# Sample attention in blocks of 16 rows by 8 columns, with queries and keys made four token tiles at a time

## The chip, the cores and the metric

The kernel runs on one core of one Trainium2 chip. The metric is device time in microseconds (us). A core has five engines that run in parallel, each with its own instruction stream in a fixed order: TensorE (PE in the profile; PEld is its weight load), VectorE (DVE), ScalarE (ACT), GpSimd (POOL) and SyncE (SP), which here only issues DMA transfers. They wait for one another through semaphores. An instruction that waits holds up everything behind it in its own stream.

## The reference

One layer of a hybrid encoder, with the same weights for a prompt of 512 tokens and a sample of 1024 tokens, model width 1024, in float32:

```python
h = rms_norm(x, norm_g)
u_pool, g_pool, q, k, v, g_attn = split(h @ w_in)          # 6 x 512 columns
pool_out = pool_mixer(u_pool, w_pool, pool_scale) * silu(g_pool)
q = rms_norm(q per head, q_norm_g) * HEAD_DIM ** -0.5       # 8 heads of 64
k = rms_norm(k per head, k_norm_g)
attn = neighbourhood_attention(q, k, v, rpb) * silu(g_attn)
y = x + concat(pool_out, attn) @ w_out
```

The neighbourhood attention sees the tokens as a grid 64 columns wide: 8 rows in the prompt, 16 in the sample. A query at row r and column c attends to 8 rows (r - 4 to r + 3, clamped at the borders) by 16 columns (c - 8 to c + 7, clamped), with a learned bias for each head, row offset (15) and column offset (31). For the prompt the 8 rows are all the rows there are.

## The kernel before

Nothing is put to an engine directly. Each operation is recorded with a priority and a modelled duration, and a planner (`Plan.order`) then lays out the fixed order of every engine: attention and evictions have priority over the long products, which run in the order of the code and fill what is left of TensorE. The planner adds a margin (`TO_PE`, 800 ns) before it counts on a result of another engine on TensorE. All instructions are issued in one place, so nearly all bear one line number; groups are told apart by the names of their tiles.

float32 values are carried as pairs of a high and a low float32r part. A product of two such pairs takes three matmuls (high by high, high by low, low by high), which is `mm3`. For the scores, queries hold the high part of a head in 64 partitions and the low part in the other 64, so two matmuls are enough: one against the high part of the keys (`k[hd]`, in both halves), one against their low part (`k[2 + hd]`).

The heads are taken in four pairs, first all of the sample, then all of the prompt. For a pair, `project_qkv` computes q, k and v token tile by token tile (128 tokens; tiles `acc`, 24 matmuls of 384 columns each). Two token tiles make a group: ScalarE brings each out of PSUM (`qkv`), the squares are summed per head, a chain of 12 small VectorE operations on `st4` (128x8) makes the reciprocal roots, q and k are scaled, TensorE transposes them into one PSUM bank (`ptq`: q in the first half, k in the second), and four evictions per head write the bank to `q` and `k`: ScalarE writes the high parts, VectorE the low parts (`low`). The sample has four such groups per pair, the prompt two. The v parts go through DRAM (`vd`) and come back as tiles of 128 keys (`vs`): for each group of 4 rows, four tiles of 4 rows by 32 columns that overlap in columns.

`attention` then runs, per head, over two query row tiles (`rt`, 8 rows each) and four column blocks (`cb`, 16 columns each): a block is 128 queries. In the sample its keys are 12 rows by 32 columns (24 at the borders, so 288 columns of scores and not 384). For each block `head_rows` does: two score matmuls (`s`); a VectorE pass that adds the bias and takes the row minimum of the negative (`ns`); ScalarE's exp with its sum; reciprocal; a scaling; three transposes (`pt`); the eviction into high and low (`pp`, two operations of 384 columns); three matmuls with v (`po`). Every two blocks the result is added up (`pv`) and multiplied into the gate (`sg`).

The bias tables are built once on GpSimd from `rpb` and stored in DRAM (`tab`). Per head and row tile they are read back with 6 or 7 DMAs, since the rows a query may see differ; the parts of the tile that no DMA writes hold -1e30 from the start. Two bias tiles are used, one for each row tile.

After the attention of a pair the rest of the pair's products follows (`accu`, `accg`: 24 matmuls of 512 columns each) and the pooling (`accm`). At the end come the output products (`acco`).

Of the kernel before, what the change touches and what calls it, by code (L numbers as in the profile page):

```python
# [24 lines left out]
P = 128  # L25
# [4 lines left out]
HD = 64  # L30
# [5 lines left out]
CT = (2, 1, 1, 0)  # L36
BANKS = dict(acc=3, s=2, pt=2, po=1)
# [301 lines left out]
def encoder(ctx, tc, xn_p, xt_p, xn_s, xt_s, w_in, w_out, w_pool, pscale, ng, qg, kg,  # L339
# [26 lines left out]
    qk_t = sb.tile([P, 2], F32, name="qk_t")  # L366
    gqk = sb.tile([P, 1], F32, name="gqk")
# [12 lines left out]

    HR = 8 * 15
    tab = dram.tile([32, HR, 32], F32, name="tab")

    def build_table():
        rel = ring("pv", 1, [P, 80], "rel")
        sp.dma_start(out=rel[0:HR, 0:48], in_=rpbm.rearrange("h r c -> (h r) c"))
        sp.dma_start(out=rel[0:HR, 48:79], in_=rpb.rearrange("h r c -> (h r) c"))

# [14 lines left out]
    def bias_rows(out, h, ro, q0, nq, a):  # L403

        o = tab.offset + (h * 15 + ro) * 32
        if nq == 1:
            sp.dma_start(out=out[16 * q0:16 * q0 + 16, :, a:a + 256],
                         in_=bass.AP(tab.tensor, o, [[HR * 32, 16], [8 * HR * 32, 3], [1, 256]]))
            return
        for ct in range(3):  # L410
            sp.dma_start(out=out[16 * q0:16 * (q0 + nq), ct, a:a + 256],
                         in_=bass.AP(tab.tensor, o + ct * 8 * HR * 32, [[32, nq], [HR * 32, 16], [1, 256]]))

    def load_bias(bt, kind, h):
        if kind == "all":
            bias_rows(bt, h, 0, 0, 8, 0)
        elif kind == "top":
            bias_rows(bt, h, 3, 3, 5, 0)
            for q in range(3):
                bias_rows(bt, h, 3, q, 1, (3 - q) * 32)  # L420
        else:
            bias_rows(bt, h, 0, 0, 4, 128)
            for q in range(4, 8):
                bias_rows(bt, h, 3, q, 1, (7 - q) * 32)
# [63 lines left out]
    ns_edge = {cb: sb.tile([P, 384], F32, name=f"ns_edge_{cb}") for cb in (0, 3)}  # L488
# [4 lines left out]
    class Sequence:  # L493


        def __init__(self, sq, S, kt_rows, hts, Rb):
            self.sq, self.S, self.kt_rows, self.hts, self.Rb = sq, S, kt_rows, hts, Rb
            self.NT, self.NB, self.CH, self.KEYS = S // P, S // 512, kt_rows // 4, kt_rows * 32
# [58 lines left out]
        def project_qkv(self, p, w, group=1):  # L557
# [3 lines left out]
            for t0 in range(0, self.NT, 2):  # L561
                st4 = ring("st4", 2, [P, 4, 8], f"st4_{sq}_{p}_{t0}")
                qkvs = []
                for t in (t0, t0 + 1):
# [28 lines left out]
                rsqrt(st4[:, 2], st4[:, 3], st4[:, 1])  # L593
                pt = bank("pt", f"ptq_{sq}_{p}_{t0}")
                for i, t in enumerate((t0, t0 + 1)):
# [7 lines left out]
                    pe.transpose(pt[:, i * P:(i + 1) * P], in_=qkv[:, 0:P], identity=ident)  # L603
                    pe.transpose(pt[:, 256 + i * P:256 + (i + 1) * P], in_=qkv[:, P:256], identity=ident)
# [4 lines left out]
                rt, r0 = (2 * t0) // 8, (2 * t0) % 8  # L609
                lo, hi = 7 - r0, 3 - r0  # L610
                qa = slice(base + rt * 512, base + (rt + 1) * 512)
                ka = slice(base + t0 * P, base + t0 * P + 256)
                own = [slice(hd * HD, hd * HD + HD) for hd in range(2)]
                k_src = [pt[own[hd], 256:512] for hd in range(2)]
                q_src = [pt[own[hd], 0:256].rearrange("p (r cb c) -> p r cb c", r=4, cb=4) for hd in range(2)]
                q_dst = []
                for hd in range(2):
                    for rows in (own[hd], own[1 - hd]):
                        v = q[hd][rows, qa].rearrange("p (cb r c) -> p r cb c", cb=4, r=8)
                        q_dst.append(v[:, lo::-1, :, ::-1] if hi < 0 else v[:, lo:hi:-1, :, ::-1])  # L620
                for hd in range(2):
                    for rows in (own[hd], own[1 - hd]):
                        act.activation(out=k[hd][rows, ka], in_=k_src[hd], func=AF.Copy, scale=gqk[own[hd]])
                    act.activation(out=q_dst[2 * hd], in_=q_src[hd], func=AF.Copy)
                for hd in range(2):
                    low(k[2 + hd][own[hd], ka], k_src[hd], k[hd][own[hd], ka], gqk[own[hd]])
                    low(q_dst[2 * hd + 1], q_src[hd], q_dst[2 * hd])
                rg = t0 // 2
                for cb in range(4):
                    sa = bass.AP(vd.tensor, vd.offset + (rg * 4 * GW + C0[cb]) * 256,  # L630
                                 [[GW * 256, 4], [256, 32], [1, 256]])
                    sp.dma_start(out=vs[base // 256 + rg][:, cb].bitcast(F32), in_=sa)
# [11 lines left out]

        def attention(self, p):
            for hd in range(2):
                for rt in range(self.NB):
                    h = 2 * p + hd
                    kind, i = (("top", 0), ("bot", 1))[rt] if self.S == 1024 else ("all", h % 2)
                    bt = bias[i][:, 0:3 * self.KEYS].rearrange("p (t c) -> p t c", t=3)  # L650
                    load_bias(bt, kind, h)
                    self.head_rows(p, hd, rt, bt)

        def head_rows(self, p, hd, rt, bt):
            sq, KEYS, base = self.sq, self.KEYS, self.base(p)
# [418 lines left out]
```

## Time and profile before

| | |
|---|---|
| Time, median of 3 runs (lowest to highest) | 648.9 us (647.37 to 649.58) |
| The profiled execution: its own time | 648.4 us |
| The profiled execution: its span | 646.6 us |
| Instructions in the span | 11390 |
| DMA, mean over the span | 157 GB/s |

The span runs from the first to the last instruction of the profile, and 1.8 us of the profiled execution's own time lie around it. Durations in the next parts are from this one execution. In a row that groups instructions, "busy" is the union of their intervals and "mean" the mean length of one. Matmuls overlap (a mean of 399 ns can go with one start every 230 ns), so what a matmul costs TensorE is read from the distance between starts. A figure after "idle" is the time for which the engine had nothing to do just before these instructions, with what ended it.

### The profile page before, as it was taken

How to read it: one execution, taken by the hardware profiler on the slowest of the kernel's cores; microseconds unless marked ns; L12 is line 12 of the kernel's file. 1: busy time of each engine (PE TensorE's matmuls, PEld its weight loads, DVE VectorE, ACT ScalarE, POOL GpSimd, SP SyncE). 2: the span in 40 equal slices, each digit the busy share in tenths (PEclk: the TensorE clock that was granted, in tenths of full speed). 3: DMA queues.
4: the chain of work that ended last, by engine and by line, in shares of the span. 5: the costliest groups of instructions: out<-in, count | busy, mean ns of one | idle time of the engine just before them, and what ended most of it. 6: DMA issues, size and time to landing. Idle time of an engine off the chain costs nothing.

```text
span 646.6 us, 11390 instructions
## 1 busy us (share of the span) xinstructions
PE 635.0 (98%) x3404; PEld 567.0 (88%) x3404; DVE 557.1 (86%) x1647; ACT 372.8 (58%) x910; POOL 100.6 (16%) x142
## 2 busy tenths in 40 slices
PE   6999999999999999999999999999999999999997
PEld 5998899988899888999889989899899878887886
DVE  6688999899987999967999989989999989879742
ACT  5766786568656476544777556477566457323210
POOL 1130100000000000101001110021212423405412
PEclk9999999999999999999999999999999999999999
DMA  8974354442274522425344355545556687843631
GB/s 304 348 205 143 104 169 124 123 121 79 59 246 137 182 62 69 134 95 152 127 112 143 109 168 162 174 139 144 169 174 195 189 261 231 269 152 118 191 131 65
DMA packets 92961, 101.53 MB, mean 157 GB/s; under 512 B 12900, under 2 KB 78564, under 8 KB 92900
## 3 DMA queue, kind: packets, MB, share of 16 engines
q1 hardware_dynamic: 92900, 100.81, 50.7%
q8 instruction: 27, 0.44, 0.3%
q14 instruction: 34, 0.28, 0.1%
HBM read 81.41 MB, written 19.37 MB: 156 GB/s over the span
## 4 chain that ended last, share of the span: by engine, by line
PE 91%; DVE 4%; DMA 3%; issue 1%; ACT 0%; SPq 0%; DVEq 0%; ACTq 0%
PE acc_s L330 21%; PE acco L330 15%; PE accg_s L330 14%; PE acc_p L330 10%; PE accu_s L330 7%; PE accg_p L330 6%; PE po_s L330 4%; PE accu_p L330 3%; PE pt_s L330 3%; PE s_s L330 3%; DMA xr<-in_xn_s 1%; PE po_p L330 1%; PE ptq_s L330 1%; DVE B L330 1%; PE pt_p L330 1%
## 5 line engine op out<-in xcount | busy, mean ns | idle before, releaser
L330 PE MATMUL acc_s<-w_sA,ht_s 128*128 128x384 f32 x768 | 145.9, 342 | 6.3 <-DVE w_sA L330 6.3
L330 PEld LDWEIGHTS acc_s<-w_sA,ht_s 128*128 128x128 f32 x768 | 136.0, 190 | 7.6 <-ACT ht_s L330 5.9
L330 PE MATMUL accg_s<-ht_s,w_sT 128*128 128x512 f32 x384 | 100.4, 399 | 0.0
L330 PEld LDWEIGHTS accg_s<-ht_s,w_sT 128*128 128x128 f32 x384 | 70.0, 188 | 12.0
L330 PE MATMUL acc_p<-w_pA,ht_p 128*128 128x384 f32 x384 | 75.4, 339 | 0.7 <-DVE w_pA L330 0.5
L330 PEld LDWEIGHTS acc_p<-w_pA,ht_p 128*128 128x128 f32 x384 | 66.1, 188 | 1.8 <-DVE w_pA L330 0.8
L330 PE MATMUL acco<-B,left 128*128 128x512 f32 x228 | 56.2, 395 | 0.6 <-DVE left L330 0.6
L330 PE MATMUL accu_s<-ht_s,w_sT 128*128 128x512 f32 x192 | 53.0, 400 | 0.0
L330 PEld LDWEIGHTS acco<-B,left 128*128 128x128 f32 x228 | 41.9, 188 | 9.5 <-DVE left L330 1.0
L330 PE MATMUL accg_p<-ht_p,w_pT 128*128 128x512 f32 x192 | 47.6, 395 | 0.0
L330 PEld LDWEIGHTS accg_p<-ht_p,w_pT 128*128 128x128 f32 x192 | 35.3, 188 | 6.9
L330 ACT ACTIVATE k<-ptq_s,gqk 64x256 fp32r<-64x256 f32 x64 | 30.1, 470 | 18.8 <-PE ptq_s L330 18.1
L330 PEld LDWEIGHTS accu_s<-ht_s,w_sT 128*128 128x128 f32 x192 | 34.6, 188 | 5.1
L330 DVE TENSOR_TENSOR xr<-acco,xr 128x512 f32<-128x512 f32 x30 | 20.5, 686 | 20.4 <-PE acco L330 18.2
L330 ACT ACTIVATE ns_edge<-ns_edge,sm_s 128x288 f32<-128x288 f32 x54 | 28.4, 529 | 16.5 <-DVE sm_s L330 16.3
L330 ACT ACTIVATE ns_s<-ns_s,sm_s 128x384 f32<-128x384 f32 x53 | 31.7, 610 | 10.1 <-DVE sm_s L330 9.9
L330 DVE TENSOR_TENSOR pp_s<-pt_s,pp_s 128x384 fp32r<-128x384 f32 x64 | 34.5, 544 | 0.3
L330 PE MATMUL po_s<-pp_s,v 128*128 128x256 f32 x192 | 32.0, 287 | 0.0
L330 PE MATMUL s_s<-k,q 128*128 128x288 f32 (+1 forms) x128 | 31.4, 330 | 0.0
L330 PEld LDWEIGHTS po_s<-pp_s,v 128*128 128x128 f32 x192 | 28.9, 188 | 1.5
L330 POOL TENSOR_TENSOR vt_s<-qkv_s,vt_s 128x128 fp32r<-128x128 f32 x17 | 9.1, 540 | 122.0 <-ACT vt_s L330 97.3
L330 ACT ACTIVATE qkv_s<-acc_s,rr_s 128x384 f32<-128x384 f32 x24 | 13.7, 578 | 23.6 <-PE acc_s L330 20.9
(221 smaller groups left out, 1350.4 us busy)
## 6 DMA issues: line engine op xcount, KB each, us to landing
v<-vd_s SPq DMA_DIRECT2D x64, 128.0 KB
wr_sA<-in_w_in SPq DMA_DIRECT2D x32, 192.0 KB
wr_sT<-in_w_in SPq DMA_DIRECT2D x32, 192.0 KB
wr_pA<-in_w_in SPq DMA_DIRECT2D x32, 192.0 KB
wr_pT<-in_w_in SPq DMA_DIRECT2D x32, 192.0 KB
out<-xr SPq DMA_DIRECT2D x24, 256.0 KB
x<-in_xt_s SPq DMA_DIRECT2D x16, 256.0 KB
vd_s<-vt_s SPq DMA_DIRECT2D x32, 128.0 KB
```

What stands on the lines that cost most here:

```text
L330: op.fn()
```

## The change

- **Blocks.** A sample block is now 16 rows (all of them) by 8 columns. Its keys are all 16 rows of the columns that its queries can see: 23 columns (368 scores) in the middle, 16 columns (256 scores) in the first and the last block. That is three chunks of 128 keys for six of the eight blocks of a head and two for the other two. Queries and keys of the sample are stored column by column, with the 16 rows innermost, so the evictions write with a step of 16 elements (64 bytes), and the keys of a block are one contiguous strip. The gate's product `sg` now runs down columns, with a step of 64 elements.
- **v.** The sample's v comes back as eight tiles of 8 columns by 16 rows that don't overlap: 8 DMAs for a pair and not 16, all of them after the last token tile. Two of the four `vs` buffers serve one pair, the other two the next.
- **Bias.** The sample has tables of its own in DRAM (`tab_s`, two of them), with a row for each query row and all masked places written out. They are built with one TensorE transpose, copies on GpSimd and 10 DMAs, 64 bytes in a run for eight of these. A head reads its bias with 3 DMAs and not 13. The tile per head alternates.
- **Groups.** q and k are made in groups of four token tiles: two PSUM banks (`qt`, `kt`), one `st4` chain of 128x16 per group, evictions of 512 elements. The sample has two groups per pair, the prompt one.
- **The rest.** `ns` tiles are four fixed ones, cleared at the start and, for two of them, again before the prompt; the bias tiles are no longer filled with -1e30 at the start; the mixed result of a head is stored with one DMA and not two. The prompt's blocks are computed as before.

```diff
+KS = 16 * 23
+EDGE = 256
...
+        rt_ps, rt = bank("pt", "rel_t"), ring("tree", 2, [P, 528], "rel_ts")
+        pe.transpose(rt_ps[0:32, 0:HR], in_=rel[0:HR, 48:80], identity=ident[0:HR, 0:HR])
+        act.activation(out=rt[0:32, 0:HR], in_=rt_ps[0:32, 0:HR], func=AF.Copy)
...
+            for dst, step, src, move, n in ((56, 15, 3, 0, 9), (192, 16, 4, 1, 4), (8, 16, 0, 1, 3)):
+                pool.tensor_copy(out=at(t, dst, [256, 2], [step, n]), in_=at(rt, 15 * h + src, [15, 2], [move, n]))
...
-            for t0 in range(0, self.NT, 2):
-                st4 = ring("st4", 2, [P, 4, 8], f"st4_{sq}_{p}_{t0}")
+            for t0 in range(0, self.NT, 4):
+                st4 = ring("st4", 2, [P, 3, 16], f"st4_{sq}_{p}_{t0}")
...
-                    pe.transpose(pt[:, i * P:(i + 1) * P], in_=qkv[:, 0:P], identity=ident)
-                    pe.transpose(pt[:, 256 + i * P:256 + (i + 1) * P], in_=qkv[:, P:256], identity=ident)
+                    pe.transpose(qt[:, i * P:(i + 1) * P], in_=qkv[:, 0:P], identity=ident)
+                    pe.transpose(kt[:, i * P:(i + 1) * P], in_=qkv[:, P:256], identity=ident)
...
+                def k_block(x):
+                    return x[:, qa] if self.S == 512 else x.rearrange("p (c r) -> p r c", r=16)[:, r0:r0 + 8]
...
+                for hd in range(2):
+                    act.activation(out=q_dst[2 * hd], in_=q_src[hd], func=AF.Copy)
+                    low(q_dst[2 * hd + 1], q_src[hd], q_dst[2 * hd])
                 for hd in range(2):
                     for rows in (own[hd], own[1 - hd]):
+                        act.activation(out=k_block(k[hd][rows]), in_=k_src[hd], func=AF.Copy, scale=gqk[own[hd]])
+                    low(k_block(k[2 + hd][own[hd]]), k_src[hd], k_block(k[hd][own[hd]]), gqk[own[hd]])
+                if self.S == 1024:
+                    if r0:
+                        for j in range(8):
+                            sa = bass.AP(vd.tensor, vd.offset + 8 * j * 256, [[256, 8], [GW * 256, 16], [1, 256]])
+                            sp.dma_start(out=vs[p % 2 * 2 + j // 4][:, j % 4].bitcast(F32), in_=sa)
...
+        def sample_block(self, p, hd, cb, bt, g):
+            first, a, n = ((0, 0, EDGE) if cb == 0 else (6, EDGE + KS, EDGE) if cb == 7 else (cb - 1, EDGE, KS))
+            ks = slice(first * P, first * P + n)
...
-                for c in range(self.CH):
-                    pe.transpose(pt[:, c * P:(c + 1) * P], in_=ns[:, c * P:(c + 1) * P], identity=ident)
+            for c in range(chunks):
+                pe.transpose(pt[:, c * P:(c + 1) * P], in_=ns[:, c * P:(c + 1) * P], identity=ident)
```

TensorE before, at the place in the second sample pair where queries and keys pass from `project_qkv` to the attention (`ptq_s_4`, `ptq_s_6`: the transposes of the third and fourth group; `s_s_0_0`, `s_s_0_1`: scores of the first two blocks; `k_94`, `k_96`: high and low part of the keys; `accg`: a long product that fills):

```order
L330 MATMUL ptq_s_4_355<-ident,qkv_s_4_350 128x128 x2
L330 MATMUL accg_s_0_0_384<-ht_s_0_111,w_sT_5_379 128x512
L330 MATMUL ptq_s_4_355<-ident,qkv_s_5_353 128x128 x2
L330 MATMUL accg_s_0_0_384<-ht_s_0_112,w_sT_6_381 128x512 x3
L330 MATMUL accg_s_0_0_384<-ht_s_0_113,w_sT_7_383 128x512 x3
L330 MATMUL accg_s_1_0_385<-ht_s_1_114,w_sT_0_369 128x512 x3
L330 MATMUL s_s_0_0_386<-k_94,q_92 128x288
L330 MATMUL s_s_0_1_391<-k_94,q_92 128x384
L330 MATMUL accg_s_1_0_385<-ht_s_1_115,w_sT_1_371 128x512 x3
L330 MATMUL accg_s_1_0_385<-ht_s_1_116,w_sT_2_373 128x512 x2
L330 MATMUL ptq_s_6_365<-ident,qkv_s_6_361 128x128 x2
L330 MATMUL ptq_s_6_365<-ident,qkv_s_7_363 128x128 x2
```

TensorE at the same place after the change (`qt_s_4`, `kt_s_4`: transposes of the second group of four token tiles; `s_s_0`, `s_s_1`: the first two blocks):

```order
L332 MATMUL kt_s_4_359<-ident,qkv_s_6_354 128x128
L332 MATMUL qt_s_4_358<-ident,qkv_s_7_356 128x128
L332 MATMUL kt_s_4_359<-ident,qkv_s_7_356 128x128
L332 MATMUL accg_s_1_0_381<-ht_s_1_119,w_sT_2_369 128x512
L332 MATMUL accg_s_1_0_381<-ht_s_1_120,w_sT_3_371 128x512 x3
L332 MATMUL accg_s_1_0_381<-ht_s_1_121,w_sT_4_373 128x512 x3
L332 MATMUL accg_s_1_0_381<-ht_s_1_122,w_sT_5_375 128x512 x3
L332 MATMUL accg_s_1_0_381<-ht_s_1_123,w_sT_6_377 128x512 x2
L332 MATMUL s_s_0_382<-k_95,q_93 128x256
L332 MATMUL s_s_1_387<-k_95,q_93 128x368
L332 MATMUL accg_s_1_0_381<-ht_s_1_123,w_sT_6_377 128x512
L332 MATMUL accg_s_1_0_381<-ht_s_1_124,w_sT_7_379 128x512
```

Before, the first scores stood between the third and the fourth group; now they stand behind the last transposes of all eight token tiles, with 12 matmuls of 512 columns in between.

ScalarE at the same place after the change (`ns_103`, `ns_104`: exp of the first two blocks):

```order
L332 ACTIVATE ze<-ze 128x512
L332 ACTIVATE q_93<-qt_s_4_358 64x8x8x8
L332 ACTIVATE k_95<-kt_s_4_359,qk_t 64x8x64 x2
L332 ACTIVATE q_94<-qt_s_4_358 64x8x8x8
L332 ACTIVATE k_96<-kt_s_4_359,qk_t 64x8x64 x2
L332 ACTIVATE ns_103,sm_s_0_383<-ns_103,sm_s_0_383 128x256
L332 ACTIVATE ns_104,sm_s_1_388<-ns_104,sm_s_1_388 128x368
```

The first scores need the first three of these evictions; before, ScalarE wrote two k parts, a q part, two k parts and a q part of 256 elements each, and the scores needed the first two of a group.

The DMA queue of SP in the same pair, before (`vd_s_327`: the pair's v in DRAM; `v_101`: tiles of v; `bias`: bias tiles, `tab`: the table):

```order
L330 DMA vd_s_327<-vt_s_6_366 128x256
L330 DMA vd_s_327<-vt_s_7_367 128x256
L330 DMA v_101<-vd_s_327 128x1x256 x4
L330 DMA bias_104<-tab 80x1x256 x3
L330 DMA bias_104<-tab 16x3x256 x3
L330 DMA bias_105<-tab 64x1x256 x3
L330 DMA bias_105<-tab 16x3x256 x4
```

And after the change:

```order
L332 DMA vd_s_325<-vt_s_6_362 128x256
L332 DMA vd_s_325<-vt_s_7_363 128x256
L332 DMA v_101<-vd_s_325 128x1x256 x4
L332 DMA v_102<-vd_s_325 128x1x256 x4
L332 DMA bias_107<-tab_71 128x1x256
L332 DMA bias_107<-tab_72 128x1x368
L332 DMA bias_107<-tab_71 128x1x256
```

All eight loads of v now stand behind the store of the last token tile, where before only the last four did; the bias of a head is three transfers.

More of the change, by code (lines that the diff above doesn't have):

```diff
@@ L365, in encoder @@
     ident = sb.tile([P, P], F32, name="ident")
-    qk_t = sb.tile([P, 2], F32, name="qk_t")
-    gqk = sb.tile([P, 1], F32, name="gqk")
+    qk_t = sb.tile([P, 3], F32, name="qk_t")
+    gqk = qk_t[:, 2:3]
     psc = sb.tile([P, NPAIR], F32, name="psc")
@@ L401, in build_table, with load_bias @@
             sp.dma_start(out=tab[16 * half:16 * half + 16].rearrange("q h c -> h q c"), in_=t)
[L403 to L408, printed above, removed]
+    def load_bias(bt, sample, h):
+        if sample:
+            for i, first, a, n in ((0, 8, 0, EDGE), (1, 0, EDGE, KS), (0, 0, EDGE + KS, EDGE)):
+                t = tab_s[i]
+                sp.dma_start(out=bt[:, a:a + n],
+                             in_=bass.AP(t.tensor, t.offset + (h * 512 + first) * 16, [[16, 8], [512, 16], [1, n]]))
             return
         for ct in range(3):
[L411 to L424, printed above, removed]
+            sp.dma_start(out=bt[:, ct * EDGE:ct * EDGE + EDGE],
+                         in_=bass.AP(tab.tensor, tab.offset + (ct * 8 * HR + h * 15) * 32,
+                                     [[32, 8], [HR * 32, 16], [1, EDGE]]))
     def split(out_h, out_l, src, scale=None):
@@ L486, in encoder @@
     vs = [ring("v", 4, [P, 4, 256], f"v_{i}", F32R) for i in range(4)]
-    ns_edge = {cb: sb.tile([P, 384], F32, name=f"ns_edge_{cb}") for cb in (0, 3)}
+    ns = [sb.tile([P, 384], F32, name=f"ns_{i}") for i in range(4)]
     bias = [sb.tile([P, 3 * 384], F32, name=f"bias_{i}") for i in range(2)]
@@ L617, in project_qkv @@
                 for hd in range(2):
                     for rows in (own[hd], own[1 - hd]):
[L619 to L632, printed above, removed]
+                        act.activation(out=k_block(k[hd][rows]), in_=k_src[hd], func=AF.Copy, scale=gqk[own[hd]])
@@ new lines, in attention @@
+                h = 2 * p + hd
+                bt = bias[h % 2]
+                load_bias(bt, self.S == 1024, h)
+                g = sg[hd * HD:hd * HD + HD, self.base(p):self.base(p) + self.S]
+                for cb in range(self.S // P):
+                    if self.S == 1024:
+                        self.sample_block(p, hd, cb, bt, g)
+                    else:
+                        self.prompt_block(p, hd, cb, bt, g)
+                sp.dma_start(out=self.mixed[4 + p, hd * HD:hd * HD + HD], in_=g)
@@ L754, in pooling @@
                 sp.dma_start(out=self.mixed[g, :, b * 512:(b + 1) * 512], in_=sgp[:, o:o + 512])
-    ss, pr = Sequence("s", 1024, 12, hts_s, Rb_s), Sequence("p", 512, 8, hts_p, Rb_p)
-    warm = sb.tile([P, 1], F32, name="warm")
-    dve.memset(warm, 0.0)
-    act.activation(out=warm, in_=warm, func=AF.Exp)
+    ss, pr = Sequence("s", 1024, hts_s, Rb_s), Sequence("p", 512, hts_p, Rb_p)
+    dve.memset(gqk, 0.0)
+    act.activation(out=gqk, in_=gqk, func=AF.Exp)
     sp.dma_start(out=g_sb, in_=ng)
@@ L779, in encoder @@
         pool.memset(k[2 + hd][HD - hd * HD:P - hd * HD].bitcast(F32), 0.0)
-    for t in ns_edge.values():
+    for t in ns:
         pool.memset(t, 0.0)
-    for bt in bias:
-        pool.memset(bt, NEG)
     for p in range(NPAIR):
```

157 lines of the change are left out of this document (92 added, 65 removed).

## The prediction

> **What bounds the kernel now.** I read first the page's busy times and the chain that ended last, then TensorE's starts in one stretch of attention, then what ended TensorE's waits.
>
> ```profile
> PE 635.0 (98%) x3404; PEld 567.0 (88%) x3404; DVE 557.1 (86%) x1647; ACT 372.8 (58%) x910; POOL 100.6 (16%) x142
> PE 91%; DVE 4%; DMA 3%; issue 1%; ACT 0%; SPq 0%; DVEq 0%; ACTq 0%
> 80.00:100.00 20.00, 20.00 (x131) 19.25 (x130) 19.94 (x63) 16.73 (x43) 0.46 (x1) 1.00 0.56 160
> ```
>
> TensorE is busy for 98% of the span and makes 91% of the chain. The third row is a window of the sample's attention (after the times: PE, PEld, DVE, ACT, POOL busy, granted clock, DMA share): the clock is 1.00, and VectorE is nearly as full (19.94 of 20.00 us) as TensorE. "Busy" for TensorE is modelled, so I check it by the distance between starts. These rows (start, length, count) are from the second sample pair:
>
> ```profile
> 145.22 0.49 PE L330 MATMUL pt_s<-ident,ns_edge 128*128 128x128 f32 x3
> 145.46 0.48 PE L330 MATMUL accu_s<-ht_s,w_sT 128*128 128x512 f32 x1
> 145.78 0.43 PE L330 MATMUL s_s<-k,q 128*128 128x288 f32 x2
> 146.05 0.49 PE L330 MATMUL pt_s<-ident,ns_s 128*128 128x128 f32 x3
> 146.29 0.94 PE L330 MATMUL accu_s<-ht_s,w_sT 128*128 128x512 f32 x3
> 147.07 0.52 PE L330 MATMUL s_s<-k,q 128*128 128x384 f32 x2
> 147.42 0.62 PE L330 MATMUL accu_s<-ht_s,w_sT 128*128 128x512 f32 x2
> 147.88 0.53 PE L330 MATMUL po_s<-pp_s,v 128*128 128x256 f32 x3
> 152.09 0.87 PE L330 MATMUL po_s<-pp_s,v 128*128 128x256 f32 x6
> 152.79 0.49 PE L330 MATMUL pt_s<-ident,ns_s 128*128 128x128 f32 x3
> ```
>
> Two `accu` matmuls take 147.88 - 147.42 = 0.46 us, 0.23 each; a pair of scores of 288 columns 0.27 (0.135 each), of 384 columns 0.35 (0.175 each); six `po` 0.70 (0.117 each). Three transposes take 0.24 to the next start, and the next matmul then comes 0.32 and not 0.23 later: 0.33 for three, **0.11 each**. No start is late, even in the middle of attention. TensorE waits only here:
>
> ```profile
> L330 PE MATMUL acc_s<-w_sA,ht_s 128*128 128x384 f32 x768 | 145.9, 342 | 6.3 <-DVE w_sA L330 6.3
> L330 PE MATMUL acc_p<-w_pA,ht_p 128*128 128x384 f32 x384 | 75.4, 339 | 0.7 <-DVE w_pA L330 0.5 <-ACT w_pA L330 0.2
> L330 PE MATMUL acco<-B,left 128*128 128x512 f32 x228 | 56.2, 395 | 0.6 <-DVE left L330 0.6
> 474.23 2.18 PE L330 MATMUL acc_p<-w_pA,ht_p 128*128 128x384 f32 x11 [0.50 <-DVE w_pA L330]
> ```
>
> 6.3 us are the first load, before any of the changed code; some 1.3 us lie far behind the sample's attention. So work taken off TensorE shortens the span by its own length, and work taken off another engine by nothing, as long as TensorE stays fed.
>
> **TensorE's sum.** Six blocks of a head keep three chunks and two have two: 8 heads x 2 = 16 transposes and 16 `po` matmuls fewer.
> - `po`: 16 x 0.117 = 1.9 us less.
> - Transposes: 16 x 0.11 = 1.8 us less.
> - Scores: 64 x 0.135 + 64 x 0.175 = 19.8 us before. After, 96 of 368 columns at 0.175 x 368/384 = 0.168 and 32 of 256 at 0.135 x 256/288 = 0.12: 19.9 us. 0.1 more.
> - One transpose more for the table: 0.1 more.
> - The transposes of q and k stay 96; only their grouping changes.
>
> In all **3.4 us less**: the profiled execution's 648.4 us (span 646.6, with 1.8 around it) become 645.0. It lies 0.5 us under the median of 648.9, so the same step from the median gives 645.5.
>
> **What becomes lighter beside it.** These rows group VectorE's and ScalarE's operations:
>
> ```profile
> L330 DVE SCALAR_TENSOR_TENSOR st_s<-st_s 128x8 f32<-128x8 f32 x96 | 16.6, 174 | 2.0
> L330 DVE TENSOR_TENSOR st_s<-st_s 128x8 f32<-128x8 f32 x48 | 8.1, 169 | 0.9
> L330 DVE SCALAR_TENSOR_TENSOR k<-ptq_s,gqk,k 64x256 fp32r<-64x256 f32 x32 | 15.4, 483 | 8.1 <-ACT q L330 7.6
> L330 DVE TENSOR_TENSOR q<-ptq_s,q 64x256 fp32r<-64x256 f32 x32 | 13.5, 422 | 0.6
> L330 DVE TENSOR_TENSOR ze<-accg_s,Rb_s 128x512 f32<-128x512 f32 x16 | 11.0, 686 | 2.3 <-PE accg_s L330 2.1
> L330 DVE TENSOR_TENSOR pp_s<-pt_s,pp_s 128x384 fp32r<-128x384 f32 x64 | 34.5, 544 | 0.3
> L330 DVE TENSOR_TENSOR sg<-pv_s,sg 64x256 f32<-64x256 f32 x32 | 13.6, 425 | 0.5
> L330 ACT ACTIVATE k<-ptq_s,gqk 64x256 fp32r<-64x256 f32 x64 | 30.1, 470 | 18.8 <-PE ptq_s L330 18.1
> L330 ACT ACTIVATE q<-ptq_s 64x256 fp32r<-64x256 f32 x32 | 12.1, 379 | 0.4
> L330 ACT ACTIVATE ze<-ze 128x512 f32<-128x512 f32 x24 | 15.1, 631 | 19.8 <-DVE ze L330 19.7
> ```
>
> The `st` chain ran 16 times for the sample; the first two rows alone are 24.7 us, and half of the runs go: 12 us less on VectorE, with the prompt's share more. An operation of 512 elements takes 686 and of 256 takes 422, so 256 elements cost 264 ns, about 1.03 ns each: two evictions of 256 joined into one save 422 x 2 - 686 = 0.16 us, and the sample's 64 become 32, 5 us less. Sixteen `pp` are a third shorter, 16 x 0.13 = 2 us. VectorE loses about 20 us or more of its 557. I count this at **nothing**: TensorE was not waiting for it.
>
> **The handover of q and k** is the step that can cost. Before, in this pair:
>
> ```profile
> 134.59 0.38 PE L330 MATMUL ptq_s<-ident,qkv_s 128*128 128x128 f32 x2
> 134.72 2.31 PE L330 MATMUL accg_s<-ht_s,w_sT 128*128 128x512 f32 x9
> 135.01 0.95 ACT L330 ACTIVATE k<-ptq_s,gqk 64x256 fp32r<-64x256 f32 x2 [2.23 <-PE ptq_s L330]
> 136.87 0.47 PE L330 MATMUL s_s<-k,q 128*128 128x288 f32 x2
> ```
>
> The transposes end at 134.97, ScalarE starts 0.04 us later, k is written at 135.96, and the scores follow at 136.87: 0.9 us to spare. Now 12 matmuls of 512 columns, 12 x 0.23 = 2.76 us, lie between the last transpose and the first scores, and these need q and two k evictions of 512 elements. A ScalarE operation gains 631 - 379 = 252 ns with 256 elements more, so these are 0.63 + 2 x 0.72 = 2.08 us. VectorE's low part of q (0.69) starts after the first and ends at 1.3. **About 0.6 us to spare**, in each of the four pairs: no wait. Behind a late eviction would stand all of ScalarE's exps of the pair and VectorE's bias passes.
>
> What I can't read from a row is the **64-byte step** of the sample's writes. The nearest row is the same operation with runs of 16 elements written backwards (`q`, 422 for 256 elements), against 425 for `sg` of the same size: no surcharge for broken runs. For the upper end I take the slowest elementwise row of the trace, GpSimd's:
>
> ```profile
> L330 POOL TENSOR_TENSOR xr<-xr,p 128x512 f32<-128x512 f32 x10 | 14.2, 1427 | 29.5 <-DVE xr L330 17.4 <-issue 11.9
> ```
>
> That is twice the 686 of VectorE. A gain is excluded, since nothing in these operations gets denser. I take no surcharge, the row it is nearest to, and keep a doubling for the range.
>
> [...]
>
> **v, bias and tables.**
>
> ```profile
> 132.34 1.44 SPq L330 DMA_DIRECT2D vd_s<-vt_s  x2
> 139.86 2.26 SPq L330 DMA_DIRECT2D v<-vd_s  x4
> 27.47 1.42 POOL L330 COPY tab<-rel 120x288 f32<-120x288 f32 x4 [23.96 <-DMA rel<-in_rpbm]
> 6.96 31.78 PE acc_s L330 x169
> L330 PE MATMUL s_s<-k,q x128: 290/338/425, 64.3 to 353.3; 128*128 128x288 f32 x64, 128*128 128x384 f32 x64
> ```
>
> The store of v ended its issue at 133.78 and its loads went out at 139.86, 6.1 us later; the last were issued by 142.12, and `po` used v at 147.88 without a wait, 5.8 us later. After the change the low part of the last v tile stands ahead of the `st` chain, two tiles' scaling, `ze` and two more: about 12 x 0.17 + 4 x 0.4 + 0.7 = 4.3 us ahead of the last transposes. The loads go out 6.1 - 4.3 = 1.8 us behind these, the first two by 2.9, and the first `po` stands some 9.8 us of matmuls behind them (in the order, from `kt_s_4` to `po_s_0`): 6.9 us, more than the 5.8 that were enough. Nothing. The bias has ten transfers fewer per head in SP's queue, and the clearing of two more `ns` tiles against that of the bias tiles falls on GpSimd, 16% busy: nothing either way.
>
> The table's transpose stands behind 127 matmuls, at about 38.7 - 42 x 0.176 = 31.3 us; its data were there at 27.4. What follows it (ScalarE, GpSimd, stores, reads) has until the first scores at 64.3, and the whole table before was ready in less. If that cover were gone, every us late would be one on the end.
>
> **The rivals.**
> 1. *The 64-byte step costs; slower.* It decides from 0.6 us / 3 evictions = 0.2 us per eviction, 40% more per element. Doubled, the chain is 2.08 + 3 x 0.50 = 3.6 us, 0.84 late plus its waits: about 0.9 x 4 pairs = 3.6 us. VectorE gets 32 evictions x 512 x 1.03 ns = 17 us and `sg` 32 x 256 x 1.03 ns = 8 us back and is as full as before; half of `sg`'s share as waits in the full windows is 4 us. 645.5 + 7.6 = 653 at the upper end, half of that, 649 to 651, for a lesser surcharge. [...] For it: each write opens new ground. Against: no row shows a surcharge on any pattern.
> 2. *The gain turns into waits, no change.* VectorE sets the pace in windows like 80 to 100, all blocks of a pair now start after the last tile, and 3 us of matmuls taken out of the cover become 3 us of waiting: 648 to 649. Against: VectorE loses more there than TensorE.
> 3. *The last waits go too.* The waits for `w_pA` and `left` come from a VectorE that is behind, and it is less behind: 1.3 to 2 us more, 643.5.
>
> **How the numbers follow.** Forecast (644.3 to 646.9) 0.48; rival 1 0.22; rival 2 0.20; rival 3 0.10. The range, 642.8 to 650.8, takes in rivals 2 and 3 and the lesser half of rival 1. About 0.3% (2 us) can be told from no change by a measurement of this kernel. Faster: 0.42 of the forecast and 0.10; same: 0.06, 0.17 of rival 2, 0.04 of rival 1; slower: 0.18 of rival 1, 0.03 of rival 2.
>
> **What would show it.** Right: PE x3373 (3404 - 32 + 1), `s_s`, `pt_s` and `po_s` without idle time, q and k evictions of 64x512 near 0.63 and 0.72 us on ScalarE and 0.7 on VectorE, `sg` still near 425 ns, VectorE under 540 us. Wrong: evictions above 0.9 us, idle time ahead of `s_s` or `pt_s`, waits of `po_s` for v, or of any matmul for `bias` by way of VectorE.

## The result, and the profile after

The changed kernel takes **667.45 us** (median of 4 runs, 663.78 to 668.74) where the kernel before took 648.6 on the same chip (647.37 to 649.58): a ratio of 1.0283, 95% interval 1.0238 to 1.0327. I had forecast 645.5 and a range up to 650.8. It is slower by some 18 us, where I had forecast a small gain, and well outside the range. The profiled execution took 667.5 us, with a span of 665.7.

The first two rows are of the page (busy times, chain that ended last), the third is the same window of the sample's attention as before:

```profile
PE 643.5 (97%) x3373; PEld 562.3 (84%) x3373; DVE 555.7 (83%) x1482; ACT 374.1 (56%) x830; POOL 91.0 (14%) x143
PE 39%; DVE 2%; DMA 1%; issue 0%; ACT 0%; ACTq 0%
80.00:100.00 20.00, 20.00 (x122) 18.23 (x121) 20.00 (x64) 17.42 (x46) 0.00 (x0) 1.00 0.38 109
```

The chain could be followed back over only 42% of the span here, so I read nothing from it. TensorE has the forecast 3373 instructions, and in the window it is as full as before. But VectorE, which should have fallen under 540 us, has 165 instructions fewer and is just as busy (555.7 against 557.1). ScalarE is busier (374.1 against 372.8) with 80 instructions fewer. So single operations have become longer. The groups by form show which (busy, mean in ns, then the idle time ahead of them and what ended it); the last four are the prompt's, with the same sizes in the same profile:

```profile
L332 ACT ACTIVATE k<-kt_s,qk_t 64x512 fp32r<-64x512 f32 x32 | 36.3, 1135 | 0.6
L332 ACT ACTIVATE q<-qt_s 64x512 fp32r<-64x512 f32 x16 | 17.4, 1090 | 6.4 <-PE qt_s L332 6.2
L332 DVE SCALAR_TENSOR_TENSOR k<-kt_s,qk_t,k 64x512 fp32r<-64x512 f32 x16 | 18.2, 1140 | 8.1 <-ACT k L332 6.9 <-PE acc_s L332 1.0
L332 DVE TENSOR_TENSOR q<-qt_s,q 64x512 fp32r<-64x512 f32 x16 | 17.3, 1084 | 6.6 <-ACT q L332 6.4
L332 DVE TENSOR_TENSOR sg<-pv_s,sg 64x256 f32<-64x256 f32 x32 | 21.6, 676 | 0.5
...
L332 ACT ACTIVATE k<-kt_p,qk_t 64x512 fp32r<-64x512 f32 x16 | 10.9, 680 | 1.3 <-DVE k L332 1.1
L332 DVE TENSOR_TENSOR q<-qt_p,q 64x512 fp32r<-64x512 f32 x8 | 5.5, 690 | 2.4 <-ACT q L332 2.2
L332 ACT ACTIVATE q<-qt_p 64x512 fp32r<-64x512 f32 x8 | 4.7, 591 | 11.0 <-PE qt_p L332 10.9
L332 DVE TENSOR_TENSOR sg<-pv_p,sg 64x256 f32<-64x256 f32 x16 | 7.2, 447 | 0.2
```

What sets the sample's operations apart from the prompt's is their step in SBUF: 64 bytes for q and k (256 for `sg`), against runs of 16 elements and more in the prompt. On ScalarE they take 1090 and not 591 ns, 1135 and not 680, on VectorE 1084 and not 690, 676 and not 447. The difference is 0.77 to 0.98 ns for each element, where an element cost about 1 ns before (1.03 on VectorE, by the prediction's rows). The whole operations take 1.5 to 1.8 times as long.

That alone would make ScalarE and VectorE busier, and TensorE is the bound. What ended TensorE's waits, by the view of the waits (us in total, times, longest; the first load and other rows of the list are left out):

```profile
PE qt_s L332 <- DVE qkv_s L332: 4.4, 5, 1.2
PE qt_s L332 <- DVE more L332: 2.4, 1, 2.4
PE s_s L332 <- DVE sm_s L332: 1.0, 3, 0.6
...
PE s_s L332 <- ACT k L332: 0.9, 3, 0.3
```

New are waits ahead of the transposes of q (`qt_s`: 6.8 us together), for VectorE's scaling, and smaller ones ahead of the scores. The timeline of TensorE in the second pair (start, length, count, idle time before):

```profile
139.72 4.36 PE L332 MATMUL accg_s<-ht_s,w_sT 128*128 128x512 f32 x18
144.86 0.30 PE L332 MATMUL qt_s<-ident,qkv_s 128*128 128x128 f32 x1 [0.78 <-DVE qkv_s L332]
...
146.72 0.27 PE L332 MATMUL kt_s<-ident,qkv_s 128*128 128x128 f32 x1
146.75 3.04 PE L332 MATMUL accg_s<-ht_s,w_sT 128*128 128x512 f32 x12
150.08 0.55 PE L332 MATMUL s_s<-k,q 128*128 128x256 f32 x2 [0.30 <-ACT k L332]
```

The 12 matmuls between the last transpose and the first scores are the cover I had counted (2.76 us), and the scores are 0.30 us late behind three evictions of 1.1 us each: this is the wait that the prediction's first rival described. The larger wait, 0.78 us, stands one step earlier, where I had not looked. The first pair shows how such a wait comes about (VectorE's timeline: `more` is a buffer that holds q, k and v of some token tiles; the last three low parts of the first four tiles are at 61.94, 63.13 and 65.45, and the scaling of the next four at 68.02; then TensorE's):

```profile
61.94 1.16 DVE L332 SCALAR_TENSOR_TENSOR k<-kt_s,qk_t,k 64x512 fp32r<-64x512 f32 x1 [0.62 <-ACT k L332]
63.13 1.09 DVE L332 TENSOR_TENSOR q<-qt_s,q 64x512 fp32r<-64x512 f32 x1
...
64.88 0.17 DVE L332 TENSOR_TENSOR st_s<-st_s 128x16 f32<-128x16 f32 x1
65.45 1.11 DVE L332 SCALAR_TENSOR_TENSOR k<-kt_s,qk_t,k 64x512 fp32r<-64x512 f32 x1 [0.39 <-ACT k L332]
...
68.02 1.43 DVE L332 TENSOR_TENSOR more<-more,st_s 128x256 f32<-128x256 f32 x4
```

```profile
61.62 4.60 PE L332 MATMUL accu_s<-ht_s,w_sT 128*128 128x512 f32 x19
68.59 0.30 PE L332 MATMUL qt_s<-ident,more 128*128 128x128 f32 x1 [2.37 <-DVE more L332]
...
70.28 3.35 PE L332 MATMUL accu_s<-ht_s,w_sT 128*128 128x512 f32 x9
```

VectorE's order was fixed beforehand: the low parts of the first group stand among the `st` chain of the second, wait there for ScalarE's evictions (0.62 and 0.39 us) and take 1.1 us each. The chain, the scaling (`more`) and TensorE's transposes all come behind them. TensorE stands for 2.37 us. The nine matmuls from 70.28 on then start 0.35 us apart in the mean (the next one starts at 73.47) instead of 0.23; the last section says why.

To put numbers on all such places I took, for every two matmuls in succession, the distance between their starts, less the usual distance for that form (0.229 us for 512 columns, 0.175 for 384 and so on); what is over by more than 0.14 us I call a late start. These are my sums over the traces, in us, with the last column for late starts ahead of `qt_s` (`ptq_s` before) and `s_s` alone. (Some matmul records are missing, which moves the first column by a few tenths.)

| kernel | usual distances | late starts | small excess | first to last matmul | late ahead of qt_s, s_s |
|---|---|---|---|---|---|
| before | 615.6 | 5.5 | 15.4 | 636.6 | 0 |
| after | 612.7 | 22.3 | 21.3 | 656.4 | 12.6 |

The matmuls themselves became 2.9 us shorter, near the 3.4 forecast. Late starts rose by 16.8 us, 12.6 of them ahead of `qt_s` and `s_s`, and the small excess rose by 5.9.

### The profile page after: what moved, and what is told of

Read it like the earlier page. It is cut to its first block, busy times and chain, and to the rows that moved or that the text cites. A ratio compares the mean times of both kernels' runs of the same rounds, so it can differ in the third digit from the quotient of the medians.

```text
span 665.7 us, 10929 instructions
## 1 busy us (share of the span) xinstructions
PE 643.5 (97%) x3373; PEld 562.3 (84%) x3373; DVE 555.7 (83%) x1482; ACT 374.1 (56%) x830; POOL 91.0 (14%) x143
## 5 line engine op out<-in xcount | busy, mean ns | idle before, releaser
L332 PEld LDWEIGHTS accg_s<-ht_s,w_sT 128*128 128x128 f32 x384 | 69.8, 188 | 13.3 <-ACT more L332 0.5
L332 PE MATMUL acc_p<-w_pA,ht_p 128*128 128x384 f32 x384 | 77.5, 343 | 0.0
L332 ACT ACTIVATE ns<-ns,sm_s 128x368 f32<-128x368 f32 (+1 forms) x110 | 60.7, 573 | 18.3 <-DVE sm_s L332 18.0
L332 PE MATMUL acco<-B,left 128*128 128x512 f32 x228 | 54.7, 392 | 0.6 <-DVE left L332 0.6
L332 PE MATMUL accu_s<-ht_s,w_sT 128*128 128x512 f32 x192 | 55.1, 411 | 0.0
L332 ACT ACTIVATE k<-kt_s,qk_t 64x512 fp32r<-64x512 f32 x32 | 36.3, 1135 | 0.6
L332 PE MATMUL s_s<-k,q 128*128 128x368 f32 (+1 forms) x128 | 33.6, 341 | 2.4 <-DVE sm_s L332 1.0
L332 DVE TENSOR_TENSOR pp_s<-pt_s,pp_s 128x384 fp32r<-128x384 f32 (+1 forms) x64 | 32.8, 513 | 0.3
L332 DVE CUSTOM_DVE_ANT_0 ns<-s_s,bias 128x368 f32<-128x368 f32 (+1 forms) x64 | 31.2, 497 | 0.2
L332 PE MATMUL pt_s<-ident,ns 128*128 128x128 f32 x176 | 30.9, 274 | 0.2
L332 PEld LDWEIGHTS s_s<-k,q 128*128 128x128 f32 x128 | 21.8, 188 | 9.3 <-DVE sm_s L332 2.8
```

Source lines behind the costliest of these rows:

```text
L332: op.fn()
```

## The experiments

Theories, in the letters that the expectations use. **A**: the 64-byte step in SBUF makes these operations about twice as long, and that is the loss. **B**: the long groups of four tiles make the hand-over too long. **O** (formed after the first four runs): the operations are longer, but the loss comes from an order that was laid out on durations without the step. **C**, where it is named, takes a step to cost as much where PSUM is read as where SBUF is written. **V** and **S** share A's loss out between VectorE and ScalarE.

**All steps moved to the PSUM side.** For q, k and the gate product, PSUM is read across and SBUF written in runs of 8 (32 bytes); the gate product takes its step out of `pv`, which is written by rows. The order of TensorE, VectorE, ScalarE and GpSimd is that of the changed kernel, instruction by instruction.

```diff
-                    return (x[:, 15:7:-1] if r0 == 0 else x[:, 7::-1])[:, :, :, ::-1]
+                    x = x[:, 15:7:-1] if r0 == 0 else x[:, 7::-1]
+                    return x[:, :, :, ::-1].rearrange("p r cb c -> p cb c r")
...
-                    return x[:, qa] if self.S == 512 else x.rearrange("p (c r) -> p r c", r=16)[:, r0:r0 + 8]
+                    return x[:, qa] if self.S == 512 else x.rearrange("p (c r) -> p c r", r=16)[:, :, r0:r0 + 8]
...
-                    k_src = [x.rearrange("p (r c) -> p r c", r=8) for x in k_src]
+                    k_src = [x.rearrange("p (r c) -> p c r", r=8) for x in k_src]
+                    q_src = [x.rearrange("p r cb c -> p cb c r") for x in q_src]
```

> The changed kernel, with the sample's q and k evictions and the gate's product turned round: PSUM is read across (step of 64 or 16 elements) and SBUF is written in runs of 8. Same values, same order on TensorE. Theory A (the 64-byte step of SBUF accesses doubles these operations, and TensorE waits for them): evictions of 64x512 fall from about 1.1 us to 0.6 to 0.75, the product from 0.67 to 0.43, the waits ahead of the q transposes and the scores go, and the time is 644 to 649 us. Rival B (groups of four token tiles make the hand-over too long): the waits stay, 660 us or more. Rival C (a step costs the same on the PSUM side): durations stay at 1.1 and 0.67, 665 us.

Measured: 649.22 us (10 runs), ratio 1.0014 to the kernel before, interval 0.9999 to 1.0028; that is at the upper end of what A had said, and far from B and C. The same groups by form:

```profile
L332 ACT ACTIVATE k<-kt_s,qk_t 64x512 fp32r<-64x512 f32 x32 | 21.8, 682 | 1.1 <-DVE k L332 0.8
L332 DVE TENSOR_TENSOR sg<-pv_s,sg 64x256 f32<-64x256 f32 x32 | 13.4, 418 | 0.5
L332 DVE SCALAR_TENSOR_TENSOR k<-kt_s,qk_t,k 64x512 fp32r<-64x512 f32 x16 | 12.0, 749 | 4.0 <-ACT k L332 3.8
L332 DVE TENSOR_TENSOR q<-qt_s,q 64x512 fp32r<-64x512 f32 x16 | 11.0, 688 | 4.1 <-ACT q L332 3.8
L332 ACT ACTIVATE q<-qt_s 64x512 fp32r<-64x512 f32 x16 | 9.4, 590 | 6.9 <-PE qt_s L332 6.7
L332 DVE TENSOR_TENSOR pv_s<-po_s,pv_s 64x256 f32<-64x256 f32 x64 | 26.1, 407 | 2.4 <-ACT pv_s L332 2.2
```

Every duration is back at the prompt's, though PSUM is now read with a step of 64 bytes and more (q, k, and `pv_s` with its 407 ns): reading PSUM so cost nothing here. TensorE's waits ahead of `qt_s` and `s_s` are gone but for one of 0.2 us. The same order with the shorter operations is about 18 us faster. A is shown in this: with the order held, the durations make the loss.

**The evictions of q and k alone** turned round, `sg` left at its step:

> As the one before, but only the q and k evictions are turned round; the gate's product keeps its step. Theory A: VectorE has 17 of the 25 us back and the chain at the hand-over is short again, so most of the loss goes: 646 to 652 us. If the product alone mattered (8 us of VectorE in full windows): 657 to 665. Rival B: 660 or more.

650.07 us (10 runs), ratio 1.0034 (1.0020 to 1.0048). So by the ratios q and k hold 16 us of the loss, and a stepped `sg` adds about 1 once these are short, although its 32 operations are 8 us longer in all (21.5 against 13.4). The two intervals overlap, so even this 1 us is barely told from nothing.

**The kernel before with groups of four**, its blocks and runs left as they were:

```diff
-            for t0 in range(0, self.NT, 2):
+            for t0 in range(0, self.NT, 4):
...
-                pt = bank("pt", f"ptq_{sq}_{p}_{t0}")
+                qt, kt = bank("pt", f"qt_{sq}_{p}_{t0}"), bank("pt", f"kt_{sq}_{p}_{t0}")
```

> The kernel before, with groups of four token tiles (two banks, one st chain of 128x16, evictions of 512 elements), its own blocks, keys, v and bias. Theory A: all writes stay in runs of 16, VectorE loses some 20 us, TensorE's matmuls are the same: 646 to 651 us. Rival B: waits ahead of the transposes and scores as in the changed kernel, 655 to 668 us.

651.85 us (6 runs), ratio 1.0051 (1.0036 to 1.0066): groups of four cost some 3 us in the old kernel, a sixth of the loss. That is a little more than A had said and less than B.

**The changed kernel with groups of two**, the steps kept:

> The changed kernel with groups of two token tiles as before: the writes keep the 64-byte step, in evictions of 256 elements. Theory A: 64-byte steps cost about 1 ns an element more at any size, so 256 elements take 0.6 to 0.75 us where they took 0.38 to 0.48; VectorE is fuller than in the changed kernel by the st chains: 660 to 675 us. Rival B: the waits go with the long group, 645 to 652 us.

672.95 us (4 runs), ratio 1.0378 (1.0358 to 1.0398): slower still. B is refuted as the main cause; with groups of two the same stepped elements pass in twice as many places.

**ScalarE's part alone, VectorE's part alone.** Runs of 8 either for the high parts (ScalarE) or for the low parts (VectorE):

```diff
-                    act.activation(out=q_dst[2 * hd], in_=q_src[hd], func=AF.Copy)
+                    act.activation(out=runs(q_dst[2 * hd]), in_=runs(q_src[hd]), func=AF.Copy)
...
-                        act.activation(out=k_block(k[hd][rows]), in_=k_src[hd], func=AF.Copy, scale=gqk[own[hd]])
+                        act.activation(out=k_runs(k_block(k[hd][rows])), in_=k_runs(k_src[hd]), func=AF.Copy, scale=gqk[own[hd]])
```

Here `runs` and `k_runs` exchange the axes to "p cb c r" and "p c r"; the second kernel has them round the arguments of the two calls of `low` instead.

> ScalarE's evictions of the sample's queries and keys (the high parts) read PSUM across and write SBUF in runs of 8; VectorE's low parts stay at the 64-byte step. Theory V (the loss sits with VectorE: its long low parts of one group stand ahead of the next group's scaling, which TensorE's transposes wait for): ScalarE's q back at 0.59 us and k at 0.68, 48 of them, yet the late starts ahead of qt_s stay and the time is 658 to 664. Theory S (it sits with ScalarE, whose evictions the scores wait for): 650 to 655. If both count by their added time (21.7 us of ScalarE's 48, 13 of VectorE's 32) it is near 657.

> The other half: VectorE's low parts of the sample's queries and keys written in runs of 8, ScalarE's evictions left at the 64-byte step. Theory V: 650 to 656, hardly a late start ahead of qt_s left, some 0.3 us ahead of s_s in the pairs. Theory S: 658 to 664. By added time alone near 660. If each half alone gives nearly all back, it is the sum of the two in one chain (high part, then low part) that overruns a cover, and not one engine.

ScalarE's alone: 655.55 us, ratio 1.0109 (1.0093 to 1.0126). VectorE's alone: 662.82, ratio 1.0220 (1.0199 to 1.0242). My theory V fails in both: ScalarE's part gives back more. S comes nearer (it holds for VectorE's part and misses ScalarE's by 0.6 us). The idle time ahead of VectorE's low parts points to why. First the kernel with ScalarE's part in runs, then the one with VectorE's:

```profile
L332 DVE SCALAR_TENSOR_TENSOR k<-kt_s,qk_t,k 64x512 fp32r<-64x512 f32 x16 | 18.4, 1152 | 1.4 <-ACT k L332 1.2
L332 DVE TENSOR_TENSOR q<-qt_s,q 64x512 fp32r<-64x512 f32 x16 | 17.4, 1085 | 2.6 <-ACT q L332 2.3
```

```profile
L332 DVE SCALAR_TENSOR_TENSOR k<-kt_s,qk_t,k 64x512 fp32r<-64x512 f32 x16 | 12.0, 750 | 14.0 <-ACT k L332 12.2 <-PE acc_s L332 1.4
L332 DVE TENSOR_TENSOR q<-qt_s,q 64x512 fp32r<-64x512 f32 x16 | 11.0, 689 | 8.4 <-ACT q L332 8.4
```

A low part can't begin before ScalarE's high part is written, and it stands in a fixed order. With its own work short and ScalarE's long, VectorE just waits there: 12.2 + 8.4 = 20.6 us, against 6.9 + 6.4 = 13.3 in the changed kernel and 7.6 with both in runs. Work and wait for ScalarE together, these low parts hold VectorE for 35.5 + 13.3 = 48.8 us in the changed kernel, 43.6 with VectorE's in runs, 39.3 with ScalarE's, 30.6 with both: 18.2, 13.0 and 8.7 above the last. By the ratios (1.0283, 1.0220, 1.0109, less 1.0034) the three lose 16, 12 and 5 us to it. The losses fall in the order of the time for which VectorE is held at the low parts, with everything queued behind them, but not in proportion to it (0.9, 0.9 and 0.6 us for each us). No run changes this time alone, so this last step is argued and not shown.

**The true durations told to the planner.** The steps stay, and in the code the table of costs alone changes. The planner uses it for the order, and also to pick the engine of those operations that more than one can do (`plan.choice`). Here `step` is that of the innermost axis of what is written:

```diff
+        step = out.ap[-1][0]
+        wide = 0.8 * n if out.space not in (PSUM, DRAM) and abs(step) >= 4 else 0
+        if wide and eng in ("scalar", "vector"):
+            return wide + Plan.narrow(eng, method, out, kw, n, aps)
```

> The writes stay as in the changed kernel; only the planner's table of costs says 0.8 ns more for each element where SBUF is written at a step of four elements or more, so that its order is built on about the true durations. Theory A (the work itself is too long for its place): 658 to 667, ACT k still near 1.13 us. Theory O (the loss is an order built on wrong durations): 647 to 653, with the late starts ahead of qt_s and s_s gone.

655.99 us, ratio 1.0116 (1.0096 to 1.0137), between the two expectations. One of its groups, and the longest of TensorE's waits behind the first load:

```profile
L341 ACT ACTIVATE k<-kt_s,qk_t 64x512 fp32r<-64x512 f32 x32 | 36.5, 1141 | 1.4 <-DVE k L341 0.7
```

```profile
PE po_p L341 <- DVE pp_p L341: 4.4, 1, 4.4
```

The evictions of k are as long as in the changed kernel, yet the waits ahead of `qt_s` and `s_s` are gone from the list. Up to 505 us of the trace, late starts and small excess (as in the table above) come to 19.1 us together, against 37.7 in the changed kernel and 19.3 with all steps moved away: up to there nothing was left of the loss against that kernel. Then TensorE waits once for 4.4 us in the last prompt pair (at 535.16), where VectorE has the conversion of loaded weights standing ahead of `pp_p`. Nothing is stepped there. Whether that wait is a chance of this order is what the next run asked, with 1.1 ns in place of 0.8:

> As told, with 1.1 ns instead of 0.8 ns for each element of a stepped write to SBUF: the same steps and the same work, another order. Told took 656 with a wait of 4.4 us of TensorE in the last prompt pair, where nothing is stepped. Theory O (an order that knows the durations hides them; that wait was a chance of the order): 649 to 653, no late start of 0.6 us or more ahead of qt_s and s_s, and no wait of 4 us. Theory A (part of the added time cannot be hidden): 655 to 660, with waits in the sample's pairs again or at other places of them.

653.26 us, ratio 1.0067 (1.0049 to 1.0085), with no wait of 4 us. Waits of 1.9 us in all ahead of `qt_s` are left, 1.7 of them at 122.80. O had said at most 653, and no late start of 0.6 us there, so it misses both marks, the first by 0.3 us, the second clearly. It still holds for most of the loss: with the same long operations, another plan brings the ratio from 1.0283 to 1.0067. The plan is more than the order, though. The pages of the two kernels (0.8 ns, then 1.1) show it:

```profile
PE 639.4 (98%) x3373; PEld 565.7 (86%) x3373; DVE 546.6 (83%) x1452; ACT 373.3 (57%) x833; POOL 123.0 (19%) x170
PE 637.5 (98%) x3373; PEld 564.2 (87%) x3373; DVE 556.1 (85%) x1460; ACT 366.3 (56%) x823; POOL 115.9 (18%) x172
```

In the changed kernel VectorE has 1482 instructions, ScalarE 830 and GpSimd 143. In all the planner has taken 30 and 22 off VectorE and given GpSimd 27 and 29 more, so what the order does and what this move does is not separated. (At 1.1 ns VectorE is as busy as in the changed kernel, 556.1 against 555.7 us.)

**A version that beats both?** Two more kernels took the strips with all steps on the PSUM side: one with groups of two everywhere, one with groups of four in the sample and of two in the prompt.

> The strips of the change, with groups of two tiles as before and all steps on the PSUM side (queries, keys, gate product in runs of 8). If the long groups cost the 3 us that the kernel before lost by them, this gives them back: 645 to 647, with TensorE's x3373 or so and about 610 us of matmuls. If groups of four only moved the same waits: 648 to 650, as with groups of four.

> All the sample's steps on the PSUM side, the sample in groups of four tiles, the prompt in groups of two as in the kernel before. If the prompt's longer group is what turns the rest of the gain into waits (the late starts of some 2 us between 515 and 590 us with groups of four): 645.5 to 647.5, ratio 0.995 to 0.999. If those waits come from any order of that stretch: 648 to 651, with late starts of the same sum at other places.

Groups of two: 651.59 us, ratio 1.0053 (1.0036 to 1.0069), slower than with groups of four and above both expectations. Mixed: 648.02 (12 runs), ratio 0.9991 (0.9981 to 1.0000), at the edge between its two expectations. The mixed one is the best form of the change and is the kernel before within 0.3%. None beats it by what can be measured.

**From which step on it costs.** Behind the kernel before, on its free bias tiles, ScalarE copies and VectorE additions of 128 elements with a step on the write (64 + step partitions) or the read (32 + step):

```diff
+                f(b[0:w, 0:n * step].rearrange("p (n s) -> p n s", s=step)[:, :, 0], a[0:w, 0:n])
+                f(b[0:r, 0:n], a[0:r, 0:n * step].rearrange("p (n s) -> p n s", s=step)[:, :, 0])
```

> The kernel before, and behind its work 112 more operations on the bias tiles: ScalarE copies and VectorE additions of 128 fp32 elements of a partition (64 at step 16), SBUF to SBUF, with the step on the write (64 + step partitions, to be told apart) or on the read (32 + step partitions), steps 1, 2, 3, 4, 6, 8 and 16 elements. If a 64-byte step costs a second cycle for each element, writes at step 16 take about 1 ns more an element than at step 1 (64 elements: some 65 ns more); the rows show from which step this begins: at 4 elements (16 bytes) or above it if neighbours within 16 or 32 bytes share an access, at 2 if any gap costs. Reads: the same, or nothing if only writes pay. The total is 10 to 30 us above the kernel before.

It ran once. The groups in the last 20 us of its trace, where ScalarE and VectorE do nothing else (so 65x128 is a write at step 1, 68x128 at step 4, 36x128 a read at step 4, and 80x64 a write of 64 elements at step 16):

```profile
L330 ACT ACTIVATE bias<-bias 72x128 f32<-72x128 f32 x2 | 0.9, 430 | 0.1
...
L330 ACT ACTIVATE bias<-bias 36x128 f32<-36x128 f32 x2 | 0.9, 426 | 0.1
...
L330 DVE TENSOR_TENSOR bias<-bias 72x128 f32<-72x128 f32 x2 | 0.8, 384 | 0.1
...
L330 DVE TENSOR_TENSOR bias<-bias 68x128 f32<-68x128 f32 x2 | 0.8, 378 | 0.1
...
L330 DVE TENSOR_TENSOR bias<-bias 36x128 f32<-36x128 f32 x2 | 0.7, 374 | 0.1
L330 DVE TENSOR_TENSOR bias<-bias 67x128 f32<-67x128 f32 x2 | 0.7, 325 | 0.1
...
L330 ACT ACTIVATE bias<-bias 80x64 f32<-80x64 f32 x2 | 0.6, 308 | 0.1
...
L330 DVE TENSOR_TENSOR bias<-bias 66x128 f32<-66x128 f32 x2 | 0.6, 290 | 0.1
L330 DVE TENSOR_TENSOR bias<-bias 65x128 f32<-65x128 f32 x2 | 0.6, 288 | 8.9 <-ACT bias L330 8.9
...
L330 ACT ACTIVATE bias<-bias 68x128 f32<-68x128 f32 x1 | 0.4, 426 | 0.0
L330 ACT ACTIVATE bias<-bias 67x128 f32<-67x128 f32 x1 | 0.4, 371 | 0.0
...
L330 ACT ACTIVATE bias<-bias 66x128 f32<-66x128 f32 x1 | 0.3, 315 | 0.0
...
L330 ACT ACTIVATE bias<-bias 65x128 f32<-65x128 f32 x1 | 0.3, 309 | 5.1 <-DVE bias L330 5.1
```

On ScalarE 309, 315, 371 and 426 ns for steps of 1, 2, 3 and 4 elements, and 430 at 8; at step 16, 64 elements take as long as 128 at step 1. VectorE: 288, 290, 325, 378, and 384 at 8. A step of 8 bytes was all but free, 12 bytes cost about half, 16 bytes the whole, and wider ones hardly more. From 1 to 4 elements ScalarE paid (426 - 309) / 128 = 0.91 ns more for each element. Reads paid like writes (at step 4, 426 ns for a read on ScalarE and 374 on VectorE).

The sums over the traces, as above, for the kernels that carry the argument (each row is of the profiled execution; that of "q and k only" took 652.7 us, 2.6 above its median):

| kernel | usual distances | late starts | small excess | first to last matmul | late ahead of qt_s, s_s |
|---|---|---|---|---|---|
| all steps on the PSUM side | 612.7 | 7.2 | 17.4 | 637.3 | 0.7 |
| q and k only | 612.7 | 10.2 | 18.5 | 641.4 | 1.6 |
| ScalarE's part only | 612.7 | 11.7 | 19.6 | 644.0 | 3.5 |
| VectorE's part only | 612.7 | 16.9 | 20.4 | 650.0 | 8.3 |
| planner told 0.8 ns | 613.1 | 14.4 | 18.1 | 645.7 | 1.3 |
| planner told 1.1 ns | 612.9 | 10.7 | 18.6 | 642.2 | 2.9 |
| mixed groups, PSUM side | 612.4 | 6.3 | 18.0 | 636.7 | 0 |

The saved matmuls (2.9 us) are there in each of them, and in none does the time fall by it. In the first row 1.7 us went into late starts (0.7 of them ahead of `qt_s` and `s_s`), 2.0 into the small excess, and the first matmul came 0.5 us earlier. Why the small excess is 2 us higher than before I can't say: it is spread over the long products, and no run tells what makes it.

## Why the prediction was wrong

The step that failed first is the last sentence on the 64-byte step: "I take no surcharge, the row it is nearest to, and keep a doubling for the range." The surcharge came, 0.77 to 0.98 ns an element. The second is the price of that doubling, 653 us at most: at 667.45 the waits that it sets off were far undersized.

- **The nearest row did not have the property in question.** `q` before wrote runs of 16 neighbours backwards, and I read its 422 ns as "no surcharge for broken runs". Broken runs were indeed free here (`q` in runs of 8: 688 ns for 512 elements, against 686 for `ze` in one run). The change has no runs at all: each element stands 64 bytes from the next. The doubling that I kept as the upper end is about what came (0.77 to 0.98 ns more an element). I gave the case 0.22.
- **Rival 1 had the cause right and the price too small.** It said 649 to 651, 653 at the upper end. Its hand-over is there, smaller than priced: 3.6 us forecast, 0.9 us of waits for ScalarE's k in three pairs, and 4.2 us of late starts ahead of `s_s` in all, with those for VectorE's bias passes. `sg`, priced at 4 us, cost about 1. What it left out is the larger part in the trace: the low parts stand ahead of the next group's scaling on VectorE, the high parts hold them up, and TensorE's transposes come late (8.3 us ahead of `qt_s`). I had written that ScalarE's exps and VectorE's bias passes stand behind a late eviction, and did not follow VectorE's stream to the next group's transposes.
- **The 20 us taken off VectorE** came as forecast where I had rows: with all steps moved VectorE is busy for 537.9 us, under the forecast 540. The `st` chain runs half as often, at 186 and 191 ns instead of 174 and 169. The 20 us were given back by the stepped operations, 12.6 us in the low parts and 8 us in `sg`.
- **TensorE's sum** was right: x3373, and 2.9 us less by the starts against 3.4.
- **"So work taken off TensorE shortens the span by its own length"** was not borne out even without the step. With all steps moved the ratio is 1.0014, and 0.9991 at best: by the number this is rival 2's outcome (648 to 649). Whether its mechanism holds is not shown: late starts rose by 1.7 us there and the small excess by 2.0, and what makes them is open.
- **v, bias and tables** cost nothing, as forecast: no matmul waits for a transfer of v or of the bias in the views of the waits above.

## What to carry to other kernels

Before pricing an eviction into a new layout, write down the innermost step on the SBUF side: at 16 bytes and more each fp32 element cost 0.7 to 1 ns more here, on top of about 1 ns, on ScalarE and VectorE, reading and writing. Turn the loops so that the step falls on the PSUM read and SBUF gets runs, since that took no more time here (590 ns on ScalarE and 688 on VectorE for 512 elements of q, against 591 and 690 in the prompt). Where the order is fixed beforehand, an operation that gets longer can cost far more than its own wait shows. Follow what is queued behind it on its own engine up to the next thing that the bound engine waits for, and correct the planner's costs with the kernel: here a plan made with nearer durations (the order, and the engine of some operations) was worth some 14 of the 18 us.

## What the hardware showed that I had not expected

Two waits of TensorE were paid twice. These are windows of the changed kernel's first pair, behind the wait of 2.37 us that ends at 68.59 (PE, PEld, DVE, ACT, POOL busy, granted clock, DMA share), and then of the kernel with the planner told 0.8 ns, at the end of its wait of 4.4 us and behind it:

```profile
69.10:72.40 3.30, 3.30 (x12) 2.73 (x11) 2.00 (x5) 1.95 (x2) 0.00 (x0) 0.50 0.53 183
72.50:73.50 1.00, 1.00 (x6) 0.78 (x5) 0.81 (x2) 1.00 (x1) 0.00 (x0) 1.00 0.01 4
```

```profile
534.50:541.10 6.60, 5.94 (x18) 4.99 (x19) 5.62 (x16) 2.63 (x7) 2.69 (x3) 0.50 0.91 279
541.30:546.00 4.70, 4.70 (x24) 3.88 (x23) 3.50 (x10) 0.69 (x2) 0.00 (x0) 1.00 0.58 191
```

After the wait of 2.37 us the granted clock was 0.50 for some 3.4 us and then 1.00 again (0.66 in the mean from 68.50 to 73.50), by my estimate another 0.34 x 5 = 1.7 us lost. At the wait of 4.4 us it was 0.50 for at least 6.6 us, about 6 of them behind the wait: another 3 us by the same estimate. It did not fall in every execution: in two of the changed kernel's four executions the mean granted clock was 1.000, in the other two 0.997. The second surprise is that PSUM could be read at steps of 64 bytes and more by ScalarE and VectorE as fast as in the prompt (590 and 688 ns for 512 elements, against 591 and 690).
